# A dilated-attention and state-space trunk: query and key projections as one Strassen product per attention unit

## The chip, the cores and the metric

The kernel runs on one core of one Trainium2 chip. Its engines have queues of their own that each run in order: TensorE (PE, with weight loads shown as PEld), VectorE (DVE), ScalarE (ACT), GpSimd (POOL) and SyncE (SP), which here issues all DMAs. The metric is the device time of one execution in microseconds (us), lower is better.

## The reference, cut to what matters

Two layers on x of 1024 tokens by 1024 channels. The first is attention in three dilation groups with a shared relative-position bias, 16 heads of 64, gated by silu; the second is a state-space layer. Both are computed in float32.

```python
DILATED_GROUPS = ((128, 1), (512, 4), (2048, 16))

def dilated_attention_mixer(h, w_in, w_out, rel_bias):
    B, S, _ = h.shape
    proj = h @ w_in                       # 1024 x (9 * 1024 + 1024)
    n_qkv = 3 * N_GROUPS_A * ATTN_WIDTH
    qkv = proj[..., :n_qkv].reshape(B, S, 3, N_GROUPS_A, ATTN_HEADS, HEAD_DIM)
    z = proj[..., n_qkv:]
    outs, lses = [], []
    for g, (window, dilation) in enumerate(DILATED_GROUPS):
        o, l = dilated_group_attention(qkv[:, :, 0, g], qkv[:, :, 1, g], qkv[:, :, 2, g],
                                       rel_bias, window, dilation)
        outs.append(o)
        lses.append(l)
    wts = jax.nn.softmax(jnp.stack(lses), axis=0)
    o = jnp.sum(wts[..., None] * jnp.stack(outs).astype(jnp.float32), axis=0)
    o = o.reshape(B, S, ATTN_WIDTH).astype(h.dtype)
    return (o * jax.nn.silu(z)) @ w_out

def reference(x, ...):
    for i in range(DEPTH):                # 2 layers: attention, then state space
        h = rms_norm(x, pre_norm)
        h = dilated_attention_mixer(h, ...) if i % 2 == 0 else s5_mixer(h, ...)
        x = x + rms_norm(h, post_norm)
    return x
```

## The kernel before

A float32 product is made of three float32r matmuls: each operand is split into a high part (a cast on ACT) and a low part (source minus high part, on DVE or POOL), and high x high, low x high and high x low are accumulated in PSUM (`split`, L88 and L89; with a scale, L91 and L92).

The stages follow each other. In the value stage (`v_phase`) the input is normalised and transposed to `hh`, `hl` (four tiles: two token halves `th` by high and low part, each with eight row blocks), and the values of all groups are projected and stored to DRAM. Five of the six value chunks go through `Quads`, a Strassen product: the input is cut into quarters (token half by row half), the sums S1 to S4 of quarters are formed once and split, and each weight chunk, cut into four quarters too, takes seven products instead of eight. Three accumulators are shared by the seven products (`ACC`), and additions between them are done on DVE.

In the attention (from about 332 to 1110 us of the profile) the loop runs over 8 pairs of heads and, within a pair, over 3 dilation groups: 24 units. A unit (`attn_pair`) loads one 128-column block of query weights and one of key weights (`load_w`: DMA to `wraw`, high part on ACT, low part on POOL, buffers `whi`, `wlo`). It projects each for both token halves (`proj_half`: 24 matmuls of 128x512 into a PSUM bank `psj`, L115), splits the banks straight from PSUM into `qh`, `ql`, `kh`, `kl` (`evac_q`, `evac_k`; two buffers each) and loads the values (`load_v`: `vp`, split to `vs`). Then come two halves u (`attn_unit`), each of four query tiles. Logits go to `psl` in blocks of two query tiles (groups 0 and 1) or four (group 2), L530, one buffer of two banks. DVE adds the bias and takes the maximum (L536, to `lg`, three buffers, each with all four tiles of a half), ACT takes the exponentials (L547), TensorE transposes the weights (L558), they are split to `ph` (three buffers), and the second matmuls (L607 for groups 0 and 1, L633 for group 2) give `pso`, which goes to `O`.

When a pair is through, its three outputs are weighted and added on POOL (`merge`, L748 and L750), during group 1 of the next pair: the softmax weights of the groups come from DRAM, broadcast to the 128 partitions (`weights_of`, `mw`, L698). POOL also computes rotation tables for the second layer (`rotations`, L1397 to L1402): three parts per pair, one per unit, each stored by two DMAs. `c.slot` hands out half-size scratch tiles from two rings, "a" with three places and "b" with four.

The order on each queue is fixed when the program is built. A planner plays the program through with costs of its own and lists for each engine what is ready by priority; `high_priority(AHEAD)` moves work 600 instructions ahead, and is used for weight loads, evacuations and the logits. Projection matmuls have no such priority and fill TensorE between the steps of the attention.

After the attention `attn_gate` projects the remaining gates from `hh`, `hl`, and `attn_out` the output; then layer 1 follows.

Of the kernel before, what the change touches and what calls it, by code (L numbers as in the profile page):

```python
# [52 lines left out]

class Ctx:
# [40 lines left out]
def load_w(c, src):  # L95

    nc = c.nc
    with c.tc.high_priority(AHEAD):
        raw = c.wraw.tile([P, KT * P], F32, tag="wraw", name="wraw")
        nc.sync.dma_start(raw, src)  # L100
        hi = c.wsp.tile([P, KT * P], F32R, tag="whi", name="whi")
        lo = c.wsp.tile([P, KT * P], F32R, tag="wlo", name="wlo")
# [199 lines left out]
class Quads:  # L302
# [4 lines left out]
    def __init__(self, c):  # L307
# [3 lines left out]
        def part(th, kh):  # L311
            return [t[:, 4 * kh:4 * kh + 4, :] for t in c.h[th]]
# [32 lines left out]
        self.tmp = t3[:, 2:4].rearrange("p a x -> p (a x)")  # L345

# [3 lines left out]
    def quad(self, raw, order, product, banks, use):  # L350
# [12 lines left out]
        def weights(i):  # L363
            with c.tc.high_priority(AHEAD):
# [13 lines left out]
                hi, lo = (c.wsp.tile([P, KT * P], F32R, tag=t, name=t)[:, 0:4 * n].rearrange("p (k x) -> p k x", k=4)  # L378
# [102 lines left out]

def load_v(c, p, g):
# [3 lines left out]
    vp = c.attn.tile([P, KT, P], F32, tag="vp", name="vp", bufs=1)  # L486
# [19 lines left out]
def attn_unit(c, g, u, q, k, v, bt, ms, O):  # L506
# [5 lines left out]
    lg = c.attn.tile([P, 2, 4, 256], F32, tag="lg", name="lg", bufs=3)  # L512
    tiles = []
    for js in ((0, 1, 2, 3),) if g == 2 else ((0, 1), (2, 3)):

        psl = c.psa.tile([P, 2, H], F32, tag="psl", name="psl")
        parts, at = [], 0
# [14 lines left out]
        for j, o, _, _ in parts:  # L532
            w = tiles[j]
            for h in range(2):
                col = ms_col(g, 0, h, u * 4 + j)
                nc.vector.tensor_tensor_reduce(  # L536
                    lg[:, h, j, 0:w], psl[:, h, o], bt[:, h, 256 - w:256], scale=1.0, scalar=-3.0e38,
# [5 lines left out]
    for h in range(2):  # L543
        for j, w in enumerate(tiles):
            col = ms_col(g, 1, h, u * 4 + j)
            b = (3 - j, j ^ 1, j)[g]
            nc.scalar.activation(lg[:, h, j, 0:w], lg[:, h, j, 0:w], AF.Exp, bias=nm[:, h, b:b + 1],  # L547
# [6 lines left out]
def transposed(c, lg, blocks, name):  # L554

    pt = c.pst.tile([P, H], F32, tag="pst", name=name)
    for n, (h, j, part) in enumerate(blocks):
        c.nc.tensor.transpose(pt[:, n * P:(n + 1) * P], lg[:, h, j, part * P:part * P + P], c.ident)  # L558
    return pt


def split_weights(c, pt, wd):
    t = c.attn.tile([P, 2, H], F32R, tag="ph", name="ph", bufs=3)
# [124 lines left out]
def weights_of(c, p, g):  # L688

    if p < 7:  # L690
        w = c.attn.tile([P, S], F32, tag="mw", name="mw", bufs=2)
    elif g:
# [9 lines left out]
def attn_pair(c, p, w_in, h):  # L702
# [3 lines left out]
    for g in range(3):  # L706
        qh = c.attn.tile([P, S], F32R, tag="qh", name="qh", bufs=2)
        ql = c.attn.tile([P, S], F32R, tag="ql", name="ql", bufs=2)
# [6 lines left out]
        kh = c.attn.tile([P, S], F32R, tag="kh", name="kh", bufs=2)  # L715
        kl = c.attn.tile([P, S], F32R, tag="kl", name="kl", bufs=2)
# [1070 lines left out]
```

## Time and profile before

| what | value |
|---|---|
| median of 3 runs | 1661.47 us (1660.74 to 1661.62) |
| profiled execution, first to last instruction | 1660.9 us; no device time of its own is given beside it |
| TensorE busy | 1640.8 us, 99% of the span |
| DVE, ACT, POOL busy | 1025.7, 710.2, 460.7 us |
| attention, one pair of heads | 97.10 us, 24 units in 8 pairs |
| chain that ended last | 76% TensorE, of it projections L115 44% |
| granted TensorE clock, mean | 0.995 |

Matmuls overlap, so their durations (about 0.4 us for 128x512) add up to more than the time they take; the pace is the distance between their starts. An idle engine costs time only where TensorE waits for it. In a row of a group the two numbers after the bar are busy time and mean duration in ns, and after the second bar stands how long the engine was idle before these instructions and who ended it.

### The profile page before, as it was taken

To read this page: it belongs to the slowest core of one execution; us is meant where nothing else is said; L and a number is where in the kernel's file an instruction comes from. 1 tells how busy PE (TensorE), PEld (TensorE's weight loads), DVE (VectorE), ACT (ScalarE), POOL (GpSimd) and SP (SyncE) were. 2 spreads that over 40 slices of the span, in tenths; PEclk is the share of its full clock that TensorE was granted. 3 is DMA by queue.
4 is the path that set the end of the run, shared out by engine and by line. 5 is a ranking of instruction groups with operands and counts; after the bars stand their busy time and mean duration, and the time that the engine had idled before them with its cause. 6 is when DMAs were issued, how large, how long until landed. Compare 5 with 4: busy or idle time off the path is not lost.

```text
span 1660.9 us, 26398 instructions
## 1 busy us (share of the span) xinstructions
PE 1640.8 (99%) x9750; PEld 1390.4 (84%) x9750; DVE 1025.7 (62%) x2515; ACT 710.2 (43%) x1732; POOL 460.7 (28%) x301
## 2 busy tenths in 40 slices
PE   8999999999999999999999999999999999999998
PEld 6889999988888888888888888888888888878886
DVE  7799999725455454545545454557564799855533
ACT  5232233326556464655645465565353132334411
POOL 1000010131342522424253252503320455422121
PEclk9999999999999999999999999999999999999999
DMA  6223455441232323324243332516336888654532
GB/s 249 70 46 108 154 172 175 139 142 55 69 103 71 104 81 92 93 64 108 71 111 87 92 106 60 150 52 192 118 121 201 245 247 242 214 190 159 159 110 87
DMA packets 176858, 212.21 MB, mean 128 GB/s; under 512 B 37443, under 2 KB 133462, under 8 KB 176728
## 3 DMA queue, kind: packets, MB, share of 16 engines
q1 hardware_dynamic: 176728, 210.52, 42.6%
q8 instruction: 77, 1.26, 0.3%
q14 instruction: 53, 0.43, 0.1%
HBM read 153.51 MB, written 56.96 MB: 127 GB/s over the span
## 4 chain that ended last, share of the span: by engine, by line
PE 76%; DVE 5%; POOL 2%; issue 1%; DMA 1%; ACT 0%; SPq 0%; DVEq 0%; POOLq 0%; ACTq 0%
PE psj L115 44%; PE pso L966 9%; PE psq L431 5%; PE psl L530 5%; PE pso L607 4%; PE pt L558 4%; PE pso L633 1%; PE psb L115 1%; DVE T L1488 1%; DVE T L1493 1%; POOL fz L923 0%; PE pv L1481 0%; PE pst L132 0%; POOL Y L1512 0%; DMA fz<-on_dr 0%
## 5 line engine op out<-in xcount | busy, mean ns | idle before, releaser
L115 PE MATMUL psj<-hh,whi 128*128 128x512 f32 x896 | 358.3, 400 | 0.0
L115 PE MATMUL psj<-hl,whi 128*128 128x512 f32 x896 | 354.9, 396 | 0.0
L115 PE MATMUL psj<-hh,wlo 128*128 128x512 f32 x896 | 349.8, 400 | 0.0
L89 POOL TENSOR_TENSOR wlo<-wraw,whi 128x1024 fp32r<-128x1024 f32 x48 | 115.3, 2401 | 396.1 <-ACT whi L88 396.1
L115 PEld LDWEIGHTS psj<-hh,whi 128*128 128x128 f32 x896 | 168.9, 188 | 36.7
L115 PEld LDWEIGHTS psj<-hl,whi 128*128 128x128 f32 x896 | 168.8, 188 | 36.1
L115 PEld LDWEIGHTS psj<-hh,wlo 128*128 128x128 f32 x896 | 168.5, 188 | 36.4
L547 ACT ACTIVATE lg<-lg,nm 128x128 f32<-128x128 f32 (+1 forms) x384 | 168.2, 443 | 37.0 <-DVE nm L542 37.0
L536 DVE CUSTOM_DVE_ANT_0 lg<-psl,T 128x128 f32<-128x128 f32 (+1 forms) x384 | 110.6, 347 | 88.8 <-PE psl L530 88.8
L88 ACT CAST whi<-wraw 128x1024 fp32r<-128x1024 f32 x80 | 83.6, 1046 | 114.7 <-PE psj L115 74.8
L431 PE MATMUL psq<-whi,v 128*128 128x256 f32 x640 | 115.4, 280 | 0.0
L89 DVE TENSOR_TENSOR kl<-psj,kh 128x512 fp32r<-128x512 f32 x48 | 33.2, 692 | 119.5 <-ACT kh L88 119.0
L89 DVE TENSOR_TENSOR ph<-pt,ph 128x512 fp32r<-128x512 f32 (+2 forms) x160 | 96.8, 622 | 15.5 <-ACT ph L88 13.5
L115 PE MATMUL psj<-h1h,whi 128*128 128x512 f32 (+1 forms) x272 | 103.9, 387 | 0.0
L115 PE MATMUL psj<-h1l,whi 128*128 128x512 f32 (+1 forms) x272 | 102.5, 381 | 0.2 <-DVE h1l L89 0.2
L88 ACT CAST ph<-pt 128x512 fp32r<-128x512 f32 (+2 forms) x160 | 81.6, 530 | 47.2 <-PE pt L558 46.3
L431 PEld LDWEIGHTS psq<-whi,v 128*128 128x128 f32 x640 | 98.4, 188 | 1.0 <-ACT whi L88 0.6
L431 PE MATMUL psq<-wlo,v 128*128 128x256 f32 x320 | 89.1, 279 | 0.0
L607 PE MATMUL pso<-ph,vs 128*128 128x256 f32 (+1 forms) x544 | 86.5, 284 | 0.0
L1344 POOL TENSOR_TENSOR Ks<-Ks,O 128x16 f32<-128x16 f32 x8 | 4.1, 508 | 288.7 <-ACT Ks L1342 275.0
L558 PE MATMUL pt<-identr,lg 128*128 128x128 f32 x560 | 82.0, 276 | 0.0
L607 PEld LDWEIGHTS pso<-ph,vs 128*128 128x128 f32 x544 | 73.5, 189 | 6.5
(282 smaller groups left out, 3632.2 us busy)
## 6 DMA issues: line engine op xcount, KB each, us to landing
wraw<-in_w_in_dram SPq DMA_DIRECT2D x56, 512.0 KB
v<-in_w_v_dram SPq DMA_DIRECT2D x24, 512.0 KB
mw<-wt_dr SPq DMA_DIRECT2D x48, 256.0 KB
vp<-v_dr SPq DMA_DIRECT2D x16, 512.0 KB
wraw<-in_ssm_w_in_dram SPq DMA_DIRECT2D x16, 512.0 KB
v_dr<-v SPq DMA_DIRECT2D x30, 256.0 KB
rot_dr<-rt SPq DMA_DIRECT2D x48, 128.0 KB
ca_dr<-ca SPq DMA_DIRECT2D x32, 144.0 KB
```

The source lines that it names most:

```text
L88: c.last_hi = nc.scalar.copy(hi, src).ins
L89: return (engine or nc.vector).tensor_tensor(lo, src, f32(hi), op=ALU.subtract)
L115: nc.tensor.matmul(ps, w[n == 2][:, k * P:k * P + P], h[n == 1][:, k, :], start=first and k == 0 and m == 0, stop=m == len(order) - 1 and ...
L431: nc.tensor.matmul(o, r[x][:, k, ts], w[y][:, k, :], skip_group_check=True, start=i in (0, 4, 5) and t % 2 == k == n == 0, stop=k == 3 and ...
L530: nc.tensor.matmul(psl[:, h, o], x[HEADS[h], qs], y[HEADS[h], ks], start=j == js[0] and n == 0, stop=n == 2, skip_group_check=True)
L536: nc.vector.tensor_tensor_reduce(lg[:, h, j, 0:w], psl[:, h, o], bt[:, h, 256 - w:256], scale=1.0, scalar=-3.0e38, op0=ALU.add, op1=ALU.ma ...
L547: nc.scalar.activation(lg[:, h, j, 0:w], lg[:, h, j, 0:w], AF.Exp, bias=nm[:, h, b:b + 1], accum_out=ms[:, col:col + 1])
L558: c.nc.tensor.transpose(pt[:, n * P:(n + 1) * P], lg[:, h, j, part * P:part * P + P], c.ident)
L607: nc.tensor.matmul(o, l, r, start=n == 0, stop=n == len(jobs) - 1, skip_group_check=True)
L633: nc.tensor.matmul(po[:, n].rearrange("p h q -> p (h q)"), vs[:, kb, x], w[:, s], start=n == 0 and m == 0, stop=n == 1 and m == 2, skip_gr ...
L966: nc.tensor.matmul(ps, x[:, k, ts], y[:, k, cols], start=n == m == 0, stop=n == KT - 1 and m == len(todo) - 1)
L1488: nc.vector.tensor_tensor_scan(T1[:, j], c.rho[:, g:g + 1].to_broadcast([P, P]), T1[:, j], 0.0, op0=ALU.mult, op1=ALU.add)
```

## The change

The query and the key block of a unit are taken as one weight matrix of 1024 x 256, cut in four (row half by query or key). `queries_keys` makes the seven products with the quarter sums S1 to S4 that the value stage has already formed; they now stay on chip through the attention (pool `pf`). A product has 4 row blocks x 3 pairs of parts. Weight differences and low parts are made on POOL. Three accumulators of one bank each take turns in the two `psj` banks. One of the four results is split from PSUM; the other three are first added on DVE into SBUF slots of ring "a".

To make room: queries and keys have one buffer instead of two, `lg` has three pieces of half the size, `ph` two buffers, the values `vp` share a ring of four with the split weights, the rotation tables are loaded in small pieces per pair and the negated part is made together with the sine part, and the merge works on half rows in ring "b". The quarter of the input that no product reads (`a21`) is stored to DRAM in the value stage and loaded back for `attn_gate` when the sums are no longer needed. Input tiles are halved into row halves (`Halves`).

```diff
+class Halves:
+    def __init__(self, low, high):
+        self.parts = low, high
+    def __getitem__(self, at):
+        p, k, cols = at
+        if isinstance(k, slice):
+            return self.parts[k.start // 4][p, :, cols]
+        return self.parts[k // 4][p, k % 4, cols]
...
 class Quads:
+        c.forms = self.rows
+        for n in range(2):
+            nc.sync.dma_start(c.a21_dr[n].rearrange("p (k x) -> p k x", k=4), f32(a21[n]))
...
+QK_ORDER = (0, 5, 1, 6, 4, 3, 2)
+def queries_keys(c, w_in, p, g, q, k):
+    nc = c.nc
+    with c.tc.high_priority(AHEAD):
+        raw = []
+        for n in range(2):
+            t = c.wraw.tile([P, KT * P], F32, tag="wraw", name="wraw")
+            nc.sync.dma_start(t, w_in[(3 * n + g) * 8 + p])
+            raw.append([t[:, x * H:x * H + H] for x in range(2)])
+        (b11, b21), (b12, b22) = raw
+        tmp = c.slot("t2", tag="b")
+    def sub(o, x, y):
+        nc.gpsimd.tensor_tensor(o, x, y, op=ALU.subtract)
+        return o
+    def weights(i):
+        with c.tc.high_priority(AHEAD):
+            if i == 5:
+                sub(b11, b12, b11)
+                x = sub(tmp, b22, b11)
+            elif i == 6:
+                x = sub(b12, b22, b12)
+            elif i == 3:
+                x = sub(b21, b21, tmp)
+            else:
+                x = {0: b11, 1: b21, 4: b11, 2: b22}[i]
+            w = c.wsp.tile([P, 2, H], F32R, tag="w", name="wqk")
+            c.last_lo = split(c, w[:, 0], w[:, 1], x, engine=nc.gpsimd).ins
+        return w
+    accs, sums = [None] * 3, {}
+    for i in QK_ORDER:
+        w = weights(i)
+        n = ACC[i]
+        if accs[n] is None:
+            accs[n] = c.psj.tile([P, H], F32, tag="psj", name="psj")
+        ps = accs[n]
+        rows = c.forms[i]
+        order = [(x, y, b) for x, y in ((0, 0), (1, 0), (0, 1)) for b in range(4)]
+        order.sort(key=lambda o: (o[1], o[2]))
+        for m, (x, y, b) in enumerate(order):
+            nc.tensor.matmul(ps, w[:, y, b * P:b * P + P], rows[x][:, b, :], start=i in (0, 4, 5) and m == 0,
+                             stop=m == len(order) - 1, skip_group_check=True)
+        with c.tc.high_priority(AHEAD):
+            if i == 0:
+                sums[0] = c.slot("p1", tag="a")
+                nc.scalar.copy(sums[0], ps)
+            elif i == 1:
+                evac_q(c, ps, g, 0, q)
+            elif i in (5, 6):
+                t = sums[i] = c.slot(f"u{i - 3}", tag="a")
+                nc.vector.tensor_tensor(t, sums[0], ps, op=ALU.add)
+            else:
+                t = sums[{4: 6, 3: 0, 2: 5}[i]]
+                nc.vector.tensor_tensor(t, t, ps, op=ALU.add)
+                if i == 3:
+                    evac_q(c, t, g, H, q)
+                else:
+                    evac_k(c, t, g, H * (i == 4), k)
...
 def load_v(c, p, g):
-    vp = c.attn.tile([P, KT, P], F32, tag="vp", name="vp", bufs=1)
+    vp = c.wsp.tile([P, KT, P], F32, tag="w", name="vp")
...
 def attn_unit(c, g, u, q, k, v, bt, ms, O):
-    lg = c.attn.tile([P, 2, 4, 256], F32, tag="lg", name="lg", bufs=3)
+    n_js = 4 if g == 2 else 2
     for js in ((0, 1, 2, 3),) if g == 2 else ((0, 1), (2, 3)):
         psl = c.psa.tile([P, 2, H], F32, tag="psl", name="psl")
+        piece = c.attn.tile([P, 4 * 256], F32, tag="lg", name="lg", bufs=3)
...
 def split_weights(c, pt, wd):
-    t = c.attn.tile([P, 2, H], F32R, tag="ph", name="ph", bufs=3)
+    t = c.attn.tile([P, 2, H], F32R, tag="ph", name="ph", bufs=2)
...
 def attn_pair(c, p, w_in):
     for g in range(3):
-        qh = c.attn.tile([P, S], F32R, tag="qh", name="qh", bufs=2)
...
-        w = load_w(c, w_in[g * 8 + p])
-        for th in range(2):
-            src = proj_half(c, w, h[th])
-            with c.tc.high_priority(AHEAD):
-                evac_q(c, src, g, th * H, (qh, ql))
+        q, k = ([c.attn.tile([P, S], F32R, tag=x + y, name=x + y, bufs=1) for y in "hl"] for x in "qk")
         bt = load_bias(c, p, g)
...
+        queries_keys(c, w_in, p, g, q, k)
...
 def merge(c, p, O):
-    for g in range(3):
-        nc.gpsimd.tensor_tensor(O[g], O[g], weights_of(c, p, g), op=ALU.mult)
+    for n in range(2):
+        cols = slice(n * H, n * H + H)
+        for g in range(3):
+            w = c.slot("mw", tag="b")
+            off = c.wt_dr.offset + (p * 3 + g) * 2048 + n * H
+            for h in range(2):
+                nc.sync.dma_start(w[HEADS[h]], bass.AP(c.wt_dr.tensor, off + h * S, [[0, 64], [1, H]]))
+            nc.gpsimd.tensor_tensor(O[g][:, cols], O[g][:, cols], w, op=ALU.mult)
...
 def attn_gate(c, a, h):
+    a21 = [row_tile(c.pa3, 1, 0, x) for x in "hl"]
+    for n in range(2):
+        nc.sync.dma_start(f32(a21[n]), c.a21_dr[n].rearrange("p (k x) -> p k x", k=4))
+    h = [h[0], [Halves(t, x.parts[1]) for t, x in zip(a21, h[1])]]
...
 def rotations(c, et, part):
+    if part == 2:
+        return
+    if part == 0:
+        t = c.attn.tile([P, 192], F32, tag="rotc", name="rotc", bufs=1)
...
     with c.tc.issue_after(c.last_lo):
-        out = c.slot("rt", tag="b")
+        out, tmp = c.slot("rt", tag="b"), c.slot("rtmp", tag="b")
...
+    if part:
+        v.tensor_scalar(tmp, out, -1.0, None, op0=ALU.mult)
+    store(part, out)
+    if part:
+        store(2, tmp)
...
-        c.wsp = pool("wsp", bufs=2)
+        c.wsp = pool("wsp", bufs=4)
```

More of the change, by code (lines that the diff above doesn't have):

```diff
@@ L100, in load_w @@
         nc.sync.dma_start(raw, src)
-        hi = c.wsp.tile([P, KT * P], F32R, tag="whi", name="whi")
-        lo = c.wsp.tile([P, KT * P], F32R, tag="wlo", name="wlo")
+        hi, lo = (c.wsp.tile([P, KT * P], F32R, tag="w", name=n) for n in ("whi", "wlo"))
         c.last_lo = split(c, hi, lo, raw, engine=c.w_engine).ins
@@ L311, in part @@
         def part(th, kh):
-            return [t[:, 4 * kh:4 * kh + 4, :] for t in c.h[th]]
+            return [t.parts[kh] for t in c.h[th]]
         add, sub = ALU.add, ALU.subtract
@@ L699, in weights_of, with attn_pair @@
     return w
-def attn_pair(c, p, w_in, h):
+def attn_pair(c, p, w_in):
     nc = c.nc
@@ L1381, in rotations @@
     v = nc.gpsimd
-    if et == part == 0:
-        f, g = c.attn.tile([P, S], F32, tag="rotf", name="rotf", bufs=1), c.slot("rotc", tag="b")
-        nc.sync.dma_start(f, c.tab_dr[:, 0:S])
-        nc.sync.dma_start(g, c.tab_dr[:, S:S + H])
-        c.rtmp = c.slot("rtmp", tag="b")
-        c.rot2 = [[t[:, n * 32 * w:(n + 1) * 32 * w].rearrange("p (k x) -> p k x", k=32) for n in range(2)]
-                  for t, w in ((f, 16), (g, 8))]
-    ps = slice(et * 4, et * 4 + 4)
-    shape = [P, 4, 8, 16]
```

85 lines of the change are left out of this document (42 added, 43 removed).

## The prediction

> **What bounds the kernel now.** First the page's engine shares and its chain, then the granted clock and busy time by stage (one attention pair per row; columns: window, its length, busy time and instructions of each engine, clock, DMA share, GB/s), then the waits of TensorE.
>
> ```profile
> PE 1640.8 (99%) x9750; PEld 1390.4 (84%) x9750; DVE 1025.7 (62%) x2515; ACT 710.2 (43%) x1732; POOL 460.7 (28%) x301
> ```
> ```profile
> 0.00:72.00 72.00, 65.21 (x274) 49.78 (x275) 51.15 (x134) 30.61 (x49) 5.15 (x7) 0.95 0.49 177
> 72.00:331.80 259.80, 258.67 (x2071) 242.32 (x2070) 233.70 (x480) 74.18 (x111) 11.65 (x16) 1.00 0.43 129
> 331.80:384.05 52.25, 52.25 (x270) 42.23 (x269) 14.26 (x47) 16.49 (x34) 18.77 (x12) 1.00 0.38 116
> ...
> 675.40:772.50 97.10, 97.10 (x599) 80.86 (x598) 50.84 (x158) 52.60 (x154) 35.12 (x19) 1.00 0.32 87
> ```
> ```profile
> PE py L1508 <- DVE X L1494: 3.7, 1, 3.7
> PE pst L132 <- issue: 3.7, 1, 3.7
> PE idle L802 <- DVE zeros L798: 1.5, 1, 1.5
> ```
> ```profile
> 331.83 27.89 PE psj L115 x120
> ```
>
> A pair (two heads, three units) takes 97.10 us and TensorE is busy for all of it, at full granted clock; of its three longest waits in the whole run none lies in the attention. DVE, ACT and POOL are at 52, 54 and 36% there. So the stage is paid in TensorE instructions, and a removed one is worth its pace, not its pipelined duration: the last row, from the chain in order of time, has 120 projection matmuls back to back in 27.89 us, 0.2324 us each.
>
> **The change part by part.** *TensorE.* A unit's query and key projections were 2 x 2 halves x 24 = 96 matmuls of 128x512. The seven products have 4 blocks x 3 hi/lo pairs = 12 each, so 84. That removes 12 x 24 units = 288 matmuls: 288 x 0.2324 = 66.9 us. A product lasts 12 x 0.2324 = 2.79 us, a unit's seven 19.5. The rest of a unit on TensorE is (97.10 - 288 x 0.2324)/3 = 10.1 us, so a pair needs 88.7 us, if the other engines keep up.
>
> *Load on the others, per pair.*
>
> ```profile
> L89 POOL TENSOR_TENSOR wlo<-wraw,whi 128x1024 fp32r<-128x1024 f32 x48 | 115.3, 2401 | 396.1 <-ACT whi L88 396.1
> L88 ACT CAST whi<-wraw 128x1024 fp32r<-128x1024 f32 x80 | 83.6, 1046 | 114.7 <-PE psj L115 74.8 <-issue 35.4 <-PE psq L431 2.8
> L88 ACT CAST ph<-pt 128x512 fp32r<-128x512 f32 x112 | 63.1, 583 | 17.8 <-PE pt L558 17.1
> L408 DVE TENSOR_TENSOR v<-v,psq 128x512 f32<-128x512 f32 x30 | 20.5, 684 | 10.6 <-PE psq L431 10.4
> L1402 POOL TENSOR_TENSOR rt<-rt,rtmp 128x512 f32<-128x512 f32 x16 | 20.8, 1303 | 1.3
> L750 POOL TENSOR_TENSOR O<-O,O 128x1024 f32<-128x1024 f32 x14 | 33.4, 2388 | 1.1
> L92 DVE SCALAR_TENSOR_TENSOR ql<-psj,qh 128x512 fp32r<-128x512 f32 x48 | 32.7, 680 | 68.1 <-ACT qh L91 68.0
> L92 DVE SCALAR_TENSOR_TENSOR y0b<-zg,y0b 128x512 fp32r<-128x512 f32 x8 | 11.1, 1384 | 2.9 <-ACT y0b L91 2.9
> ```
> ```profile
> L88 ACT CAST g0b<-gy x8: 616/620/622, 1441.6 to 1480.3; 128x512 fp32r<-128x512 f32 x8
> ```
>
> POOL loses 6 splits of 2.40 us (14.4) and gains 21 splits and 12 subtractions of 128x512, at 1.30 (the rt row) 42.9; the merge's halves cost 6 x 1.30 instead of 3 x 2.39, +0.6. 35.1 becomes 64.2 us, 72% of 88.7. ACT loses 6 x 1.046 and gains 21 x 0.62 and three PSUM copies of 0.58: 52.6 becomes 61.0, 69%. DVE gains 15 adds of 0.684 (10.3), and nine of the twelve lo parts of queries and keys are now taken from an SBUF sum instead of PSUM. The same instruction costs 0.680 us from PSUM (ql) and 1.384 from SBUF beside a working POOL (y0b, layer 1), so between 0 and 0.7 each, 0 to 6.3: 50.8 becomes 61 to 67, at most 76%. No engine passes TensorE; what can go wrong is latency.
>
> *What the 1.384 is.* Three timeline rows: start, duration, engine.
>
> ```profile
> 675.17 2.03 DVE L542 TENSOR_SCALAR nm<-ms 128x8 f32<-128x8 f32 x1
> ```
> ```profile
> 672.32 4.86 POOL L750 TENSOR_TENSOR O<-O,O 128x1024 f32<-128x1024 f32 x2
> ```
> ```profile
> L542 DVE TENSOR_SCALAR nm<-ms x48: 158/172/2031, 369.9 to 1115.4; 128x8 f32<-128x8 f32 x48
> ```
>
> An SBUF-only DVE instruction with a median of 0.172 us took 2.03 and ended at 677.20, when POOL's two additions ended (672.32 + 4.86 = 677.18): it stood until POOL was through. With POOL at 72% this meets three lo parts a unit. The one that matters is the last key half, ahead of the unit's first logits: exposed in full it is 24 x 0.7 = 17 us, hidden it is nothing. In front of it stand two of the next unit's products (5.6 us of TensorE work) against add 0.68, hi 0.62, lo 0.68 to 1.38, that is 2.0 to 2.7 us; so it is nearer hidden, and I take 0.25 us a unit, 6 us. The Trainium skill (SBUF — State Buffer, "Who interferes with whom") says that a DVE instruction with two SBUF inputs and a GpSimd instruction that reads SBUF exclude each other for a whole instruction; by that rule taken alone the term would be the 17 us, by the cover in front of it nothing. The rows above agree with the rule.
>
> *One buffer for queries and keys (two before).* The next unit's first evacuation (third product) must wait for this unit's last logits; with two banks for three accumulators the fifth product then waits too. So TensorE can run four products ahead, 11.2 us, no more. How long until the last logits?
>
> ```profile
> 679.07 0.39 PE L530 MATMUL psl<-kl,qh 64*128 64x256 f32 x2
> ...
> 679.90 1.37 PE L607 MATMUL pso<-ph,vs 128*128 128x256 f32 x10
> ...
> 685.26 0.38 PE L530 MATMUL psl<-kl,qh 64*128 64x256 f32 x2
> ...
> 698.32 0.39 PE L530 MATMUL psl<-kl,qh 64*128 64x256 f32 x2
> ```
> ```profile
> 681.13 0.08 DVE L536 DVE_READ_ACCUMULATOR2_ANT ms<- 128x1 f32 x1
> ...
> 715.84 0.29 DVE L536 CUSTOM_DVE_ANT_0 lg<-psl,T 128x128 f32<-128x128 f32 x1 [1.34 <-PE psl L530]
> ...
> 723.72 0.29 DVE L536 CUSTOM_DVE_ANT_0 lg<-psl,T 128x128 f32<-128x128 f32 x1 [2.73 <-PE psl L530]
> ```
> ```profile
> L536 DVE CUSTOM_DVE_ANT_0 lg<-psl,T 128x256 f32<-128x256 f32 x176 | 65.4, 418 | 53.4 <-PE psl L530 53.4
> ```
>
> A unit of groups 0 and 1 has four blocks of logits, each 0.83 us of TensorE (679.07 to 679.90) and read by DVE by 681.21, so a turn can be 2.1 us. Today's turns are (698.32 - 679.07)/3 = 6.4 us. Low end: 2.0 + 3 x 2.1 + 0.8 = 9 us after the last product; TensorE has 11.2 + 4 x 0.83 = 14.5 us of work, no idle. High end: 2.0 + 19.3 + 0.8 = 22.1 us against 14.5 and half of the unit's other work, (10.1 - 3.3)/2 = 3.4: 4.2 us idle. I take the low end: in today's turns DVE waits for TensorE (53.4 us in the last row), because 14 to 18 projection matmuls stand between two blocks; the order makes the spacing, not the latency. Group 2 has two blocks, 7.9 us apart (723.72 - 715.84): 10.7 us, covered either way.
>
> *The rest.* Logits in halves (three half pieces for three whole ones) and two weight buffers for three: the third block's softmax must be out of a piece before the second unit half reuses it; both are behind products, 0, without that cover part of the 4.2 above. The ring of four weight tiles holds values too; weights for product five wait for product one, 1.9 us of split against 8.4 us of products, 0. Raw query and key weights come as a pair, freed after the last split at about 3 x 2.79 + 1.9 = 10.3 us into a unit, needed at 29.6: 2 x 512 KB at the rate below is 4.4 us, 0 in steady state; in the first unit, with no attention to cover it, the chain (10.3 + 4.4, some 2 to land, 6.4 for the first two weights = 23) passes the second product of unit 1 at 22.3: I take 2 us (0 to 5). Storing one row quarter (2.1 MB) lies in the value stage with its DMA share of 0.43: 0. Loading it back is
>
> ```profile
> GB/s 7 241 223 133 0 0 0 0 12 170 301 70 0 0 0 39 184 111 3 0 0 118 208 2 213 14 0 0 69 239 150 1 139 255 162 17 218 197 0 0
> ```
>
> 8.7 us at 241 GB/s, beside the last three products (its place is that of a sum last read by the fourth) and the first gate half (24 x 0.2324 = 5.6): 2 us (0 to 8.7). Rotations: seven POOL instructions a pair as before, two small loads more, the negated part now in group 1's unit.
>
> *SP and POOL queues at the merge.*
>
> ```profile
> 753.72 8.69 SPq L698 DMA_DIRECT2D mw<-wt_dr  x6
> 763.69 0.34 SPq L100 DMA_DIRECT2D wraw<-in_w_in_dram  x1
> ```
>
> Six weight rows hold SP 8.69 us today with a projection load behind them. After, twelve issues share a ring of four with the weight differences and also wait for POOL's products (6 x 1.30): about 13 us, against 19 between the raws' release and their use. Covered, 0.
>
> Sum, on the profiled span: 1660.9 - 66.9 + 6 (lo part) + 2 (first unit) + 2 (reload) = 1604.0. The page gives no time of its own for the profiled execution beside its span; the median of the runs is 0.6 above the span, so 1605.
>
> **The rivals.** *B, the merge unit.* In group 1's unit POOL has 11 x 1.30 = 14.3 for weights, 5 for four rotation instructions, 6 x 1.30 + 2 x 2.39 = 12.6 for the merge (2.6 more from the fifth merge on): 32 to 34.5 us in a unit of 29.6, in order, and the second weight of the next unit needs a ring place that the merge frees. If four weight tiles of lead do not absorb it, 2.3 to 4.9 us a pair, with as much again from loads queued on SP behind it and from DVE waiting on POOL: 8 x 2.3 to 8 x 6 = 18 to 48 us back, 1620 to 1650; 1632 in the middle. For it: POOL doubles. Against: the other two units leave it 15 us each.
>
> *C, slower.* The single buffer idles TensorE by the high end above: 16 units of groups 0 and 1 x 4.2 = 67 us, which with the 10 us of the sum ends at 1605 + 67 = 1672. It decides from (66.9 - 10)/16 = 3.6 us of idle per such unit on. For it: today's spacing is 6.4 us. Against: that spacing is order. The Trainium skill (TensorE: Matmul & The Clock Gate, "Part 1: The HAM clock gate (the "warmup" mystery)") puts a re-throttled clock behind idle times of about 3.4 us. Gaps of C's size would then cost more than themselves; in this trace the attention has no gap and 1.00 throughout, so no row tells.
>
> *D, a unit-wide latency of a bit of everything* (ACT and DVE in order at 70 to 76%): 0.5 us in each unit is 12 us, 1617. It shades A.
>
> **How the numbers follow.** A, TensorE stays the bound, 1595 to 1618 (every small term at nothing: 1594.6; with D 1617): 0.52, forecast 1605. B, 1618 to 1657: 0.27. C, 1665 and more: 0.18. About no net change: 0.03. Signs are mixed but A and B hold most; A's own range is 1595 to 1618. The range 1595 to 1660 leaves out C and a little below. What a measurement of this kernel can tell from no change is 0.2%, 3.3 us. Faster 0.79, same 0.03, slower 0.18.
>
> **What would show it.** Right: 84 matmuls of 128x512 per unit at 0.232 us, pairs of 89 to 90 us, TensorE idle in the attention below 1 us a unit, POOL near 64 us a pair. B: a gap once a pair, weights waiting for a POOL difference or split behind the merge. C: gaps of 3 to 4 us before the fifth product in groups 0 and 1, released by the evacuation of the third. The lo part: key or query lo rows of 1 us and more that end with a POOL instruction. Wrong altogether: a pair above 97 us with few gaps, which would mean slower matmuls.

## The result, and the profile after

| | median | range | against before |
|---|---|---|---|
| before | 1661.11 us | 1660.58 to 1661.62 | |
| after | 1682.08 us | 1679.05 to 1685.29 | 1.0124 [1.0108, 1.0141] |

The change is 1.2% slower, beyond the upper end of the range (1660), where 1605 was forecast. The profiled execution took 1679.76 us, its span is 1678.0.

The engine shares of the page after:

```profile
PE 1603.8 (96%) x9462; PEld 1352.1 (81%) x9462; DVE 1160.8 (69%) x2635; ACT 792.8 (47%) x1876; POOL 723.0 (43%) x541
```

TensorE has the 288 matmuls less (9750 to 9462), but it is no longer busy 99% of the time. Granted clock and busy time by stage, columns as in the prediction: first two stages, then two pairs from the middle and the last pair:

```profile
0.00:72.00 72.00, 63.91 (x272) 49.20 (x273) 50.49 (x134) 29.99 (x49) 5.23 (x7) 0.91 0.56 206
72.00:337.40 265.40, 263.25 (x2073) 246.65 (x2072) 234.21 (x480) 74.41 (x112) 13.85 (x19) 1.00 0.42 127
...
595.80:695.50 99.70, 93.22 (x582) 76.18 (x580) 68.14 (x175) 63.82 (x173) 69.65 (x49) 1.00 0.29 86
695.50:795.00 99.50, 91.31 (x548) 74.49 (x549) 67.25 (x172) 62.32 (x170) 66.08 (x49) 0.98 0.28 86
...
992.70:1101.90 109.20, 99.13 (x577) 80.73 (x576) 70.35 (x180) 65.41 (x184) 70.92 (x52) 0.92 0.29 87
```

The pair of the fourth row takes 99.5 us; a pair took 97.10 before, and 88.7 were expected. TensorE is idle for 8.2 us of it (99.50 - 91.31). Pairs differ, from 95.1 to 109.2 us; the seven from 398.7 to 1101.9 take 100.5 in the mean, with 6.9 idle. POOL, ACT and DVE are within a few us of the loads that the prediction gave them (64.2, 61.0, 61 to 67), so no engine became the bound by its sum. The value stage ends 5.6 us later than before (337.4 instead of 331.8).

TensorE's waits after (total us, times, longest):

```profile
PE pso L696 <- ACT ph L101: 12.4, 13, 2.9
PE psj L545 <- ACT wqk L101: 10.0, 9, 1.8
PE pso L696 <- DVE ph L102: 9.9, 12, 1.8
PE pt L647 <- ACT lg L636: 7.2, 9, 2.1
...
PE psl L619 <- DVE kl L102: 3.4, 5, 1.1
```

Before, none of the three longest waits lay in the attention. Now there are many, up to 2.9 us, on several steps, about 50 us in all. No step waits in every unit. One wait repeats from pair to pair: a product has stood 1.4 us for a weight when it starts at 518.81, 617.93, 717.05 and 815.02. POOL is idle then (it had waited 5.85 us for ACT at 717.07); ACT comes late to the cast, behind exponentials, a key part and a copy. Another wait can be followed through the four engines in the timeline after (start, duration, engine, and in brackets the idle time before it).

```profile
690.87 2.29 POOL L516 TENSOR_TENSOR wraw<-wraw,t 128x512 f32<-128x512 f32 x1
693.11 2.35 POOL L831 TENSOR_TENSOR O<-O,O 128x1024 f32<-128x1024 f32 x1
695.43 3.75 POOL L102 TENSOR_TENSOR wqk<-wraw,wqk 128x512 fp32r<-128x512 f32 x3
```
```profile
693.15 2.35 DVE L631 TENSOR_SCALAR nm<-ms 128x8 f32<-128x8 f32 x1
```
```profile
693.19 1.14 ACT L101 CAST wqk<-wraw 128x512 fp32r<-128x512 f32 x2 [3.33 <-POOL wraw L516]
695.53 0.51 ACT L636 ACTIVATE lg<-lg,nm 128x256 f32<-128x256 f32 x1 [1.21 <-DVE nm L631]
```
```profile
693.85 0.28 PE L619 MATMUL psl<-kh,qh 64*128 64x128 f32 x2
696.19 0.71 PE L647 MATMUL pt<-identr,lg 128*128 128x128 f32 x3 [2.06 <-ACT lg L636]
697.06 0.71 PE L647 MATMUL pt<-identr,lg 128*128 128x128 f32 x3 [0.16 <-ACT lg L636]
697.53 0.53 PE L545 MATMUL psj<-hh,wqk 128*128 128x512 f32 x1
697.86 0.63 PE L545 MATMUL psj<-hl,wqk 128*128 128x512 f32 x1
698.29 0.63 PE L545 MATMUL psj<-hh,wqk 128*128 128x512 f32 x1
```

DVE's negated maximum (`nm`, 0.172 us in the median before) stands until POOL's addition in the merge ends: 693.15 + 2.35 = 695.50, 693.11 + 2.35 = 695.46. The exponentials on ACT wait for it, 1.21 us longer than ACT's own work before them, and TensorE, whose queue has the transposes next and the product behind them, is idle for 2.06 us. The prediction showed the same event before (2.03 us at 675.17). There TensorE ran projection matmuls meanwhile and lost nothing. And the weights of the next product waited too: ACT stood 3.33 us for a weight difference on POOL. Then the product runs with its matmuls 0.43 us apart (697.86 to 698.29) instead of 0.232. The clock of that stretch:

```profile
694.00:698.00 4.00, 1.78 (x12) 1.04 (x9) 3.19 (x10) 2.79 (x12) 4.00 (x4) 0.98 0.41 132
698.00:702.00 4.00, 4.00 (x12) 2.87 (x10) 1.02 (x2) 1.88 (x8) 1.18 (x1) 0.60 1.02 314
702.00:706.00 4.00, 4.00 (x34) 3.61 (x34) 1.79 (x3) 2.66 (x5) 1.88 (x2) 1.00 0.20 82
```

In slices of 1 us the same stretch reads 0.50 in its middle:

```profile
697.00:698.00 1.00, 0.94 (x5) 0.70 (x6) 0.20 (x2) 1.00 (x6) 1.00 (x2) 0.91 0.94 259
698.00:699.00 1.00, 1.00 (x4) 0.80 (x3) 0.00 (x0) 1.00 (x6) 1.00 (x1) 0.50 0.84 248
701.00:702.00 1.00, 1.00 (x5) 0.55 (x3) 0.00 (x0) 0.00 (x0) 0.00 (x0) 0.89 1.01 332
```

So this gap is paid twice: 2 us idle, and then 3.4 us at half clock. Not every gap is: by such slices the attention of this execution has seven half-clock stretches, of 3.4 or 6.8 us, behind more than fifty waits; before, it had none. They are 34 us in all and can cost 17. Over the run the mean granted clock went from 0.995 to 0.984; 0.011 x 1678 = 18 us bounds what that can cost. The Trainium skill (TensorE: Matmul & The Clock Gate, "Part 1: The HAM clock gate (the "warmup" mystery)") says that the clock is halved after an idle window of about 3.4 us. The trace agrees on the halving (0.50), but here 2.06 us of idle, in a stretch of 4 us with 1.78 us of work, were enough.

### The profile page after: what moved, and what is told of

The parts are those of the page before. It is cut to its first block, busy times and chain, and to the rows that moved or that the text cites. A ratio compares the mean times of both kernels' runs of the same rounds, so it can differ in the third digit from the quotient of the medians.

```text
span 1678.0 us, 26619 instructions
## 1 busy us (share of the span) xinstructions
PE 1603.8 (96%) x9462; PEld 1352.1 (81%) x9462; DVE 1160.8 (69%) x2635; ACT 792.8 (47%) x1876; POOL 723.0 (43%) x541
## 3 DMA queue, kind: packets, MB, share of 16 engines
q8 instruction: 74, 1.21, 0.3%
## 4 chain that ended last, share of the span: by engine, by line
PE 51%; DVE 11%; DMA 7%; ACT 6%; POOL 6%; issue 3%; SPq 1%; DVEq 0%; ACTq 0%; POOLq 0%
PE psj L545 15%; PE psj L127 12%; PE pso L1055 9%; PE psq L446 4%; ACT lg L636 3%; PE psl L619 3%; POOL wqk L102 2%; PE pt L647 2%; DMA wraw<-in_w_in_dram 2%; PE pso L696 2%; PE pso L722 1%; PE psb L127 1%; DMA vp<-v_dr 1%; DVE lg L625 1%; DVE kl L102 1%
## 5 line engine op out<-in xcount | busy, mean ns | idle before, releaser
L545 PE MATMUL psj<-v,wqk 128*128 128x512 f32 x1152 | 301.9, 405 | 3.9 <-ACT wqk L101 3.1
L102 POOL TENSOR_TENSOR wqk<-wraw,wqk 128x512 fp32r<-128x512 f32 x144 | 197.6, 1381 | 214.4 <-ACT wqk L101 209.5
L545 PEld LDWEIGHTS psj<-v,wqk 128*128 128x128 f32 x1152 | 211.8, 191 | 48.9 <-ACT wqk L101 3.6
L545 PE MATMUL psj<-hh,wqk 128*128 128x512 f32 x576 | 202.8, 410 | 9.3 <-ACT wqk L101 6.9
L545 PEld LDWEIGHTS psj<-hh,wqk 128*128 128x128 f32 x576 | 108.8, 193 | 35.9 <-ACT wqk L101 9.6
L101 ACT CAST wqk<-wraw 128x512 fp32r<-128x512 f32 x144 | 87.3, 618 | 99.8 <-PE psj L545 46.0
L102 DVE TENSOR_TENSOR kl<-u,kh 128x512 fp32r<-128x512 f32 x48 | 64.6, 1346 | 76.6 <-ACT kh L101 76.5
L545 PE MATMUL psj<-hl,wqk 128*128 128x512 f32 x288 | 116.7, 405 | 0.0
L1082 POOL TENSOR_TENSOR xr<-xr,y 128x512 f32<-128x512 f32 x30 | 38.2, 1295 | 126.4 <-DVE y L1081 99.2
L101 ACT CAST whi<-v 128x1024 fp32r<-128x1024 f32 x35 | 36.7, 1050 | 109.4 <-PE psq L446 91.4
```

What stands on the lines that cost most here:

```text
L101: c.last_hi = nc.scalar.copy(hi, src).ins
L102: return (engine or nc.vector).tensor_tensor(lo, src, f32(hi), op=ALU.subtract)
L545: nc.tensor.matmul(ps, w[:, y, b * P:b * P + P], rows[x][:, b, :], start=i in (0, 4, 5) and m == 0, stop=m == len(order) - 1, skip_group_c ...
L1082: nc.gpsimd.tensor_tensor(x[:, ns], x[:, ns], y, op=ALU.add)
```

## The experiments

All times are medians; the ratio is to before, run on the same chip. "Old buffers" means two buffers for queries and keys, six half pieces for `lg` and three buffers for `ph`.

**Is the first term right?** Before, with 12 of the 96 matmuls of a unit left out and nothing else changed.

```diff
-    order = [(k, n) for k in ks for n in range(3)]
+    order = [(k, n) for k in ks for n in range(3) if not (short and k < 3 and n == 1)]
```


> The kernel before with 12 of each unit's 96 projection matmuls left out (low x high of three row blocks, result differs) and nothing else changed: 288 matmuls fewer. My first term, 288 x 0.2324 = 66.9 us: 1594. If the old buffers and engines have no slack for a shorter unit either: 1600 to 1630.

1597.4 us, 0.9618 [0.9603, 0.9632]: 63.7 us less, against 66.9 in the sum. The gain is there to be had, so the change lost 1682.1 - 1597.4 = 84.7 us elsewhere. In this kernel TensorE has no idle time and no half clock in the attention. In the profile of the change the two come to about 50 and up to 17 us, most of the loss.

**The buffers alone.** First the halved buffers with the projections of before, then the same with two buffers for queries and keys.

```diff
-        queries_keys(c, w_in, p, g, q, k)
+        w = load_w(c, w_in[g * 8 + p])
+        for th in range(2):
+            src = proj_half(c, w, h[th])
+            with c.tc.high_priority(AHEAD):
+                evac_q(c, src, g, th * H, q)
...
```


> Before's projections (96 matmuls a unit, evacuated from PSUM, no sums kept) with the halved attention buffers, the merge in half rows, and the new rotations. Buffer theory: the halved buffers cost the 77 us that the attention lost against my sum, so 1661 + 77, about 1740; at least 1690. Side-engine theory (sums evacuated from SBUF, weights made late on POOL): the buffers cost next to nothing, 1655 to 1670.

1753.9 us, 1.056 [1.0544, 1.0575].

```diff
-        q, k = ([c.attn.tile([P, S], F32R, tag=x + y, name=x + y, bufs=1) for y in "hl"] for x in "qk")
+        q, k = ([c.attn.tile([P, S], F32R, tag=x + y, name=x + y, bufs=2) for y in "hl"] for x in "qk")
```


> e1 (before's projections, halved buffers, 1754) with queries and keys in two buffers again. If the single query and key buffer is the mechanism of my slower rival: back near 1665. If the softmax pieces and split weights carry it: 1735 or more.

1667.7 us, 1.0042 [1.0027, 1.0057]. With the old projections the single query and key buffer is worth 86 us and the rest of the halving 7 us. So rival C's buffer costs even more here than C gave it (86 against 67), but by other waits than C's gaps of 4.2 us: with the single buffer no wait of the attention is above 1.6 us, and the mean granted clock there (330 to 1190 us) is 0.95 against 1.00 with two. Nor does the size carry over to the products, as the next runs show.

**The buffers under the products.** The sums S1 to S4 are not kept: the products read the quarters themselves in the same number and shape. On this base the old buffers are given back in parts.

```diff
-        c.forms = self.rows
-        for n in range(2):
-            nc.sync.dma_start(c.a21_dr[n].rearrange("p (k x) -> p k x", k=4), f32(a21[n]))
+        c.forms = [a11, a12, a22, a22, a11, a12, a11]
```


> Control for e2, e5, e6 and e7: the change with its own buffers, with quarters in place of the sums (nothing kept, stored or loaded back; result differs). What keeping the sums costs outside the attention: 5 us of the value stage, up to 5 at the reload, so 1672 to 1677; e2 and e7 are then 23 to 28 and 7 to 12 us of buffers. If keeping the sums costs nothing: 1682.

1673.6 us, 1.0079 [1.0064, 1.0094]: keeping the sums costs 8.5.

> e2 with only the query and key buffers doubled; softmax pieces and split weights stay at the change's three and two. If the single query and key buffer is what the buffers cost, as my slower rival had it: as e2, 1649. If the softmax pieces are: near 1672, the change less the 6 to 10 us that e2 saves outside the attention.

(`bufs=2` for queries and keys on that base.) 1665.1 us, 1.0021 [1.0011, 1.003]: 8.5 us, not 67.

```diff
-        piece = c.attn.tile([P, 4 * 256], F32, tag="lg", name="lg", bufs=3)
+        piece = c.attn.tile([P, 4 * 256], F32, tag="lg", name="lg", bufs=6)
...
-    t = c.attn.tile([P, 2, H], F32R, tag="ph", name="ph", bufs=2)
+    t = c.attn.tile([P, 2, H], F32R, tag="ph", name="ph", bufs=3)
```


> e10 (quarters in place of the sums, 1674, result differs) with six softmax pieces and three split-weight buffers, queries and keys still single. With e7 (queries and keys double, 1665) and e2 (all, 1649): if the two parts add, 1674 - (1665 - 1649) = 1658. If softmax buffers help only with double queries and keys: 1670 or more.

1653.6 us (seven runs, 1645.9 to 1660.1), 0.9966 [0.995, 0.9981]: 20 us, more than the queries and keys.

> The change's products with the buffers of before for queries and keys (2), softmax (six pieces) and split weights (3). To make room the seven products read quarters of the input in place of the four sums, so that the sums need no place: the number of instructions is the change's, the result differs. Buffer theory: about 1605. Side-engine theory: 1665 to 1685, as the change.

(Both.) 1649.3 us, 0.9925 [0.991, 0.994]: 24.3 us for all buffers. The products with old buffers are faster than before, but only by 12 us of 64.

**POOL.** No weight differences, and the low part of a weight replaced by the high part: no weight work on POOL.

```diff
-        nc.gpsimd.tensor_tensor(o, x, y, op=ALU.subtract)
-        return o
+        return x
...
-            c.last_lo = split(c, w[:, 0], w[:, 1], x, engine=nc.gpsimd).ins
+            c.last_lo = c.last_hi = nc.scalar.copy(w[:, 0], x).ins
...
-            nc.tensor.matmul(ps, w[:, y, b * P:b * P + P], rows[x][:, b, :], start=i in (0, 4, 5) and m == 0,
+            nc.tensor.matmul(ps, w[:, 0, b * P:b * P + P], rows[x][:, b, :], start=i in (0, 4, 5) and m == 0,
```


> The change without POOL's eleven instructions a unit: no weight differences, and the low part of a weight replaced by its high part (result differs, same matmuls). POOL-weights theory, late weights and DVE held up by POOL: 1630 or less. Evacuation theory: half of its loss goes with the POOL instructions that held up DVE, about 1655. Buffer theory: above 1675.

1631.8 us, 0.9817 [0.9801, 0.9833]: 50 us less than the change. `nm` by shape, in this kernel and in the change:

```profile
L630 DVE TENSOR_SCALAR nm<-ms 128x8 f32<-128x8 f32 x48 | 10.1, 210 | 0.3
```
```profile
L631 DVE TENSOR_SCALAR nm<-ms 128x8 f32<-128x8 f32 x48 | 29.2, 609 | 0.6
```

> The old buffers of e2 (quarters in place of the sums) and POOL's weight instructions left out as in e4. If the two causes are all there is, and they add: 1594 to 1605, the matmuls' own time. If a third cause is left (sums evacuated from SBUF, strided): 1610 to 1625.

(The same with old buffers and without the sums.) 1618.8 us, 0.9748 [0.9705, 0.9792]: 30.5 less than with old buffers alone. Is it that POOL is busy, or that its results come late? POOL gets its instructions back, on scratch tiles that nothing waits for.

```diff
+            for _ in range({5: 3, 6: 2, 3: 2}.get(i, 1)):
+                nc.gpsimd.tensor_tensor(c.busy[0], c.busy[1], c.busy[2], op=ALU.subtract)
```


> As e5, but POOL gets its eleven 128x512 instructions a unit back, on scratch tiles whose results nothing reads (a weight's low part is still its high part). Late-weights theory (TensorE waits for what POOL makes): as e5. Occupancy theory (POOL's work holds DVE and the merge up, whoever reads it): as e2, 1649.

1636.7 us, 0.9848 [0.9833, 0.9863]. Of the 30.5 us, 17.9 come back with a busy POOL that delivers nothing. (The runs without POOL's work spread from 1614 to 1629, so the split is known to some 7 us.) The other 12.6 could be weights that come late, but that is not shown: with old buffers and POOL's weights TensorE's waits in the attention name the side engines' work on weights `ph` and keys `kl`, and none of them a weight `wqk`:

```profile
PE pso L694 <- DVE ph L102: 13.3, 12, 1.2
PE psl L617 <- DVE kl L102: 8.2, 7, 1.3
PE pso L694 <- ACT ph L101: 6.4, 6, 1.1
```

Nor does the busy POOL stand beside as much of DVE's work: 35 of 48 low key parts overlap one of its instructions, against 46 when it makes the weights. In the change itself, with the halved buffers, TensorE did wait 10.9 us for weights (10.0 on ACT's part, 0.9 on POOL's).

**Where the query and key parts are read from.** First from PSUM for all, without the SBUF sum.

```diff
-                    evac_q(c, t, g, H, q)
+                    evac_q(c, ps, g, H, q)
-                    evac_k(c, t, g, H * (i == 4), k)
+                    evac_k(c, ps, g, H * (i == 4), k)
```


> The change, but the three sums, though still added on DVE, are not used: queries and keys are split from the PSUM bank instead of the SBUF sum (result differs). Side-engine theory with the evacuation as its cause (lo parts 1.34 us instead of 0.69, strided high parts 1.2 instead of 0.59): 1640 or less. Buffer theory: above 1675. POOL-weights theory: above 1670.

1682.7 us, 1.0124 [1.0089, 1.0159]: no gain. The reads are short again (low key parts 0.691), but the bank now stays taken until the low part is done. TensorE's waits of this kernel:

```profile
PE psl L619 <- DVE ms L625: 13.5, 7, 4.1
PE psj L545 <- ACT wqk L101: 10.0, 6, 2.3
PE psj L545 <- DVE kl L102: 7.2, 12, 1.0
PE psj L545 <- DVE u L555: 6.6, 7, 1.5
```

In the change no wait of a product for a bank (the last two rows) is above 1 us in total, and none for `ms` above 0.3. So one wait went and others came, and this run says nothing of the lo parts by itself. What it hid was found in the durations of the high part. Tile rows of the change (min/median/max in ns):

```profile
L104 ACT ACTIVATE qh<-psj x24: 573/592/601, 345.8 to 1102.5; 128x512 fp32r<-128x512 f32 x24
L104 ACT ACTIVATE qh<-p x24: 625/1180/1220, 356.8 to 1111.4; 128x512 fp32r<-128x512 f32 x24
L101 ACT CAST kh<-u x48: 612/1110/1224, 352.1 to 1120.3; 128x512 fp32r<-128x512 f32 x48
L102 DVE TENSOR_TENSOR kl<-u,kh x48: 728/1198/2152, 352.7 to 1121.6; 128x512 fp32r<-128x512 f32 x48
```

The same in the run above in which POOL makes no weights:

```profile
L101 ACT CAST kh<-u x48: 614/1127/1258, 351.1 to 1066.1; 128x512 fp32r<-128x512 f32 x48
L102 DVE TENSOR_TENSOR kl<-u,kh x48: 679/1174/2391, 351.7 to 1067.2; 128x512 fp32r<-128x512 f32 x48
```

ACT's 1.1 us is there with and without POOL's work, so it is no lock. In groups 1 and 2 `evac_q` and `evac_k` take every 4th or 8th element of the source ("p (l r) -> p r l"). From PSUM that costs nothing (0.592); from SBUF the same read takes twice as long. The next edit lets the sums be written in the order of the split, so that the strided read is that of PSUM.

```diff
-                nc.scalar.copy(sums[0], ps)
+                nc.scalar.copy(rl(sums[0]), lr(ps))
-                nc.vector.tensor_tensor(t, sums[0], ps, op=ALU.add)
+                nc.vector.tensor_tensor(rl(t), rl(sums[0]), lr(ps), op=ALU.add)
...
+    src = t.rearrange("p (r l) -> p r l", r=ORD[g])
+    split(c, hi, lo, src[:, :, ::-1] if scale else src, scale)
```


> The change with the three sums kept in the order that queries and keys are stored in, so that their split reads SBUF in one run; the strided read is moved to PSUM. Same result as the change. If the strided SBUF read is what makes the high part 1.2 us on ACT: high parts back at 0.62 us, lo parts at 0.7 plus POOL's share, and, if DVE and ACT latency counts, 1665 to 1675. If it does not count: 1680, same as the change.

1661.7 us, 1.0000 [0.9986, 1.0014]: 20.4 us less than the change. Its tile rows:

```profile
L101 ACT CAST kh<-u x48: 602/617/623, 348.9 to 1103.4; 128x512 fp32r<-128x512 f32 x48
L102 DVE TENSOR_TENSOR kl<-u,kh x48: 680/910/1854, 349.5 to 1104.0; 128x512 fp32r<-128x512 f32 x48
```

ACT is back at 0.617, DVE's low part at 0.91, not 0.69, because POOL is still busy: the 37 low key parts that overlap a POOL instruction have a median of 1.14, the 11 others 0.69. In the change, with the strided read, the two are 1.57 (38) and 1.11 (10).

> Old buffers and no POOL weight instructions as in e5 (result differs), and the sums in split order as in e8. If buffers, POOL and the strided read are all the causes: 1594 to 1603. If something else is left: 1610 or more.

(Order, old buffers, no POOL weights, sums not kept.) 1608.7 us, 0.9687 [0.9673, 0.9702]. Now the low part is short as well, and no wait of the attention is left above 1.3 us:

```profile
L101 ACT CAST kh<-u x48: 602/617/623, 348.4 to 1044.6; 128x512 fp32r<-128x512 f32 x48
L102 DVE TENSOR_TENSOR kl<-u,kh x48: 682/692/1781, 349.0 to 1045.2; 128x512 fp32r<-128x512 f32 x48
```

**Why keeping the sums costs.** The value stage ends 5.6 us later than before, with a store as the only thing added there. The chain in order of time, the same stretch of 63 matmuls in before, after, and the run without the sums:

```profile
265.05 7.17 PE psq L431 x63
```
```profile
267.97 7.47 PE psq L446 x63
```
```profile
264.59 7.17 PE psq L444 x63
```

0.1138 us for each 128x256 matmul against 0.1186, with no wait. The instructions are the same; what differs in the kernel after is where their tiles lie, and the store. Without the sums and the store, but with the value stage's tiles in the new pool, which is closed ahead of the attention:

```diff
-        c.vslot = lambda n, dt: pool.tile([P, 4, H], dt, tag=f"v{n}", name=f"v{n}")
+        c.vslot = lambda n, dt: (pool if n in (2, 3, 10, 11) else c.pf).tile([P, 4, H], dt, tag=f"v{n}", name=f"v{n}")
...
+    c.es_pf.close()
```


> e10 with the value stage's tiles in the places that the change gives them (its left pool), but nothing stored and nothing kept in the attention (result differs as e10's). If the place of the tiles makes the value stage longer: its matmuls of 128x256 at 0.118 us instead of 0.114, the stage ends some 4 us later than e10's. If the store of 2 MB does: no difference from e10.

1680.1 us in a single run, and in its chain

```profile
266.43 7.47 PE psq L444 x63
```

Its value stage ends at 335.4, against 331.3 without the sums. The slower pace comes with the placement alone, without the store. Which property of the placement it is was not found.

**Is there a version that beats both?** On the sums in split order, low parts of some weights go from POOL to DVE. Products run in the order 0, 5, 1, 6, 4, 3, 2.

```diff
-            c.last_lo = split(c, w[:, 0], w[:, 1], x, engine=nc.gpsimd).ins
+            c.last_lo = split(c, w[:, 0], w[:, 1], x, engine=nc.vector if i in (0, 1) else nc.gpsimd).ins
```


> e8 with the low part of the first and third weight of a unit (products 0 and 1) made on DVE instead of POOL, same result as the change. POOL loses 2 x 1.38 us a unit, 8.3 a pair, and its first difference starts earlier; DVE gains 2 x 0.64 to 1.0, 4 to 6 a pair. If late weights are the larger part of POOL's cost: 1645 to 1655. If DVE's queue is what counts: 1662 to 1675.

1650.3 us, 0.9946 [0.9927, 0.9966].

> e12 (1650) with a third of the seven low parts, that of the last product, on DVE as well; same result as the change. Lateness theory: the last product's weight is the least urgent, so 1648 to 1654. Occupancy theory: another 4 us a pair off POOL, 1640 to 1646.

(0, 1 and 2.) 1665.9 us, 1.0031 [1.0017, 1.0045].

> e8 (1662) with only the first product's low part on DVE, same result as the change. Lateness theory: the first weight opens the unit and lets POOL start the differences of the second, so most of e12's 11 us: 1650 to 1656. Order theory (the planner's order changes with every such edit, and the time with it, whatever moves): anywhere from 1650 to 1668.

(Only 0.) 1660.9 us, 1.0005 [0.9995, 1.0016].

> e8 with the low parts of the first and second products (0 and 5, the two that must be ready when a unit opens) on DVE, same result as the change. Lateness theory: better than e12, 1640 to 1650. Order theory: anywhere from 1645 to 1668.

(0 and 5, the first two.) 1648.1 us, 0.9926 [0.9909, 0.9942]: the fastest version with the reference's whole computation, 13 us below before and 34 below the change. The series is not monotone: none, one, two and three low parts give 1661.7, 1660.9, 1648.1 or 1650.3, and 1665.9. The lateness theory is not borne out by the traces: TensorE's waits for ACT's part of a weight are 14.0, 17.9, 18.3 or 20.6, and 18.1 us, no shorter in the two good ones. With each edit the planner also writes another order. What made the two good ones good stays open. This wait stands out in the version with 0 and 1:

```profile
PE psj L560 <- ACT wqk L101: 20.6, 8, 4.2
```

Eight times in eight pairs, up to 4.2 us. From the second pair on it comes 94 to 98 us apart (481.13, 575.05, 670.15 and so on). In the one at 670.15 the weight differences stand among the merge's products on POOL, and ACT waits for one of them:

```profile
666.43 1.28 POOL L844 TENSOR_TENSOR O<-O,mw 128x512 f32<-128x512 f32 x1 [1.35 <-DMA mw<-wt_dr]
667.67 1.26 POOL L525 TENSOR_TENSOR t<-wraw 128x512 f32<-128x512 f32 x1
668.96 0.62 ACT L101 CAST wqk<-t 128x512 fp32r<-128x512 f32 x1 [3.62 <-POOL t L525]
670.15 0.79 PE L560 MATMUL psj<-hh,wqk 128*128 128x512 f32 x1 [2.86 <-ACT wqk L101]
```

That is rival B's mechanism, once a pair; all four versions of the series that use DVE have it.

**The ladder.** From the change down, in one order of removal:

| kernel | median | step |
|---|---|---|
| the change | 1682.1 | |
| sums not kept | 1673.6 | 8.5 |
| and old buffers | 1649.3 | 24.3 |
| and no weight work on POOL | 1618.8 | 30.5 |
| and sums in the split's order | 1608.7 | 10.1 |
| before with 84 matmuls | 1597.4 | 11.3 |

The steps overlap: alone, taken from the change, POOL is worth 50 us and the order 20. The last 11.3 are not assigned. The two have 9462 matmuls each, with no wait above 1.3 us in the attention of the first. In the profiled executions they are 16.0 us apart in device time (1611.55 and 1595.51), and 7.2 of these lie behind the last matmul of the attention's output (420.0 against 412.8 us to the end), in the second layer, which takes 413.1 with old buffers alone. Why stays open.

## Why the prediction was wrong

- **The first term holds.** 84 matmuls of 128x512 run in 19.5 us when nothing disturbs them, as the chain after shows in the first unit, and 63.7 of 66.9 us were measured by themselves.

```profile
337.40 19.52 PE psj L545 x84
```

- **The loads hold, the conclusion does not; this is the step that failed.** "No engine passes TensorE; what can go wrong is latency" named the right place, and then the forecast put every such latency at nothing or next to it, and D gave half a us per unit. The idle 8.2 us of the pair shown are 2.7 a unit (2.3 in the mean of seven pairs), about five times that, with the clock on top: about 50 us of idle and up to 17 of half clock in the attention, where D had 12. TensorE's queue is in order, and three engines at 62 to 70% work in a chain (add, high, low; difference, high, low; maximum, exponential, transpose, split), so over fifty times in 24 units a step came late. The mechanism was right and its size was wrong by the whole gain.
- **The lock was priced in one place only.** The prediction found `nm` standing 2.03 us behind POOL, and then charged it only on the last key half (6 us). A POOL that is busy costs 17.9 us with nothing waiting for it, and POOL's weight work 30.5 in all; "weights for product five wait for product one, 1.9 us of split against 8.4 us of products, 0" took the best case. The size was low too: the 1.384 us beside a working POOL is a mean over two kinds, as the tile row of before shows. Three of the eight overlap no POOL instruction and take 0.69; the five that do take 1.78 to 1.82.

```profile
L92 DVE SCALAR_TENSOR_TENSOR y0b<-zg,y0b x8: 686/1781/1822, 1496.1 to 1563.0; 128x512 fp32r<-128x512 f32 x8
```

The rule cited there from the Trainium skill (SBUF — State Buffer, "Who interferes with whom") holds in this row and in the low key parts, which have two SBUF inputs. The `nm` rows that the prediction set beside it have one, so they do not bear on that rule. The page names their kind too: the `nm` form (a tensor with a scalar) can enter a mode with two ports and then locks as well.
- **A read that was not checked for its pattern.** The prediction compared ql from PSUM (0.680) with a contiguous SBUF row (1.384) and put the whole difference to POOL. Two things lie in it here. Without POOL's weight work the strided low part takes 1.1 to 1.2; with the order mended and POOL busy 0.91; with both gone 0.69. And ACT's high part was priced at 0.62 from a contiguous row and took 1.1 to 1.2. That is 3 reads in each unit of groups 1 and 2, six a pair, which the prediction did not have as longer. The Trainium skill states it (SBUF — State Buffer, "Door 1: The DMA port swizzle (why `[64,N]` ≈ `[32,N]`)"): lines of 16 bytes, with a penalty for each access that crosses to a new one. A stride of four float32 or more, 16 bytes, then meets a new line at each element. The durations agree, 0.617 against 1.18. The page counts strides of up to 4 float32 as free; this trace does not agree: the key part takes 1.12 at a stride of 4 (group 1) and 1.19 at 8 (group 2). The PSUM read with the same stride took 0.592.
- **"Logits in halves ... 0".** The halved softmax pieces cost 20 us, by the run that gives them back. For queries and keys the measured 8.5 us are nearer the low end (0) than the high one (67); here 0 was wrong. The cover named was products, and these were waiting themselves; that this is why is argued, not shown.
- **The value stage, "0".** 5.6 us later, with a slower matmul pace; the placement alone gave 4.1 us in a single run. The prediction looked at DMA and not at where tiles lie.
- **The rivals.** C's outcome is nearest in time (1672 forecast, 1682 measured), but by luck: there is no 4.2-us gap before the fifth product, and two buffers give back 8.5. B's gap behind the merge is not among the waits of the change that repeat; it stands out in the version with two low parts on DVE. What the change lost is a sum of small things (buffers, a busy POOL, the strided read, the kept sums), of which the prediction had only D, to "shade" A. Half-clocked matmuls behind gaps were named under C, as what a gap would cost beyond itself, and are in the trace.

## What to carry to other kernels

When the bound engine loses 9% of a stage's work (66.9 of 8 x 97.1 us), the others must be that much earlier in every step and not only in their sums: halve buffers and load a helper engine in separate versions, and time each before they are put together. Price a moved read by a row with the same memory, the same stride and the same neighbour at work. A saved copy or buffer that leaves 2-us gaps on TensorE costs the gap and can cost a slower clock behind it.

## What the runs showed of the hardware that was not expected

- ACT's cast of 128x512 from SBUF takes 0.617 us contiguous (median) and 1.12 when every 4th, 1.19 when every 8th element is read; from PSUM the strided read takes 0.592. DVE's subtraction of the same size goes from 0.692 to about 1.1, and to 1.57 where POOL works beside it.
- A DVE instruction of 128x8 (0.172 us) took up to 2.35 us beside a POOL addition and ended with it.
- The same 128x256 matmuls went 0.1138 or 0.1186 us apart depending on the pool that their tiles were in.
- After 2.06 us of idle the granted clock fell to 0.50 for 3.4 us, 1.6 us after work had begun again.
